# A two-layer decoder trunk on one core: a prefetch hint for the jump over a rarely taken branch, and another order of the expert groups around it

## The chip, the cores and the metric

The kernel runs on one core of a Trainium2 chip. The metric is the time of one execution in device microseconds (us); lower is better. The core has TensorE (PE for matmuls, PEld for the weight loads that run beside them), VectorE (DVE), ScalarE (ACT), GpSimd (POOL) and SyncE (SP); DMA queues move data between main memory and the on-chip memory.

## The reference

`reference()` runs two decoder layers over 256 tokens of width 1024 in float32. Layer 0 mixes tokens with a Mamba-2 block, layer 1 with block-sparse attention; neither is touched here. After each mixer comes the PEER channel mixer, and then a layer norm and a gated add:

```python
q = (xb @ w_q).reshape(PEER_TOKEN_BLOCK, PEER_HEADS, 2, PEER_HALF)
s = jnp.einsum('thcd,hcnd->thcn', q, sub_keys).astype(f32)
...                       # top 16 of 128 keys, twice; top 16 of their 256 sums
u_g = u[expert]
v_g = v[expert]
act = jax.nn.gelu(jnp.einsum('td,thkd->thk', xb, u_g).astype(f32))
return jnp.einsum('thk,thkd->td', (gate * act).astype(v_g.dtype), v_g)
...
x = layer_norm(alpha * x + ffn, ln_ffn_g[i], ln_ffn_b[i])
gate = jax.nn.sigmoid((x @ ple_w_gate[i]).astype(jnp.float32)).astype(x.dtype)
x = x + gate * (p[i] @ ple_w_proj[i])
```

Each layer has 16384 experts (a table u for the way in and a table v for the way out), and each token uses 8 x 16 of them.

## The kernel before

All of it is unrolled Python in a class `Net`; a tile framework turns data dependences into semaphores, and each engine runs its own instructions strictly in the order in which they were put on its queue. The change lies in the last part of `peer(i)`, which runs once for each layer.

**How the experts are worked.** The 16384 experts are 128 *columns* of 128. For every column, `expert_in` multiplies the tokens with the whole of u. The weights of the columns are kept in main memory (`table`; `first` holds those of the first block of tokens alone) for columns 0 to 95, and on the chip (the tile `high`) for columns 96 to 127. For the way out, columns 96 to 127 are *dense*: `dense(e)` takes column e of v by a plain DMA on SP's queue (512 KB) and multiplies it with the weights of all 256 tokens, 12 matmuls. Of columns 0 to 95 only the experts that some token uses are worked: they are sorted into *groups* of 128 rows, and `group(s)` fetches the rows of v and of the weight table by two indirect DMAs on POOL's queue (`fetched`). There are 84 groups: 38 whose experts are used by both blocks of 128 tokens (kind 0, the list `both`, 12 matmuls), 23 for the first block alone (kind 1, `one`, 6 matmuls) and 23 for the second alone (kind 2, `two`, 6 matmuls). The last five of `two` form the list `last` and are worked at the very end, so that the first block's layer norm can run beside them.

**What a column or a group costs.** float32 is multiplied as a high and a low part: `split` has ACT cast the high part (`hi`) and DVE subtract it for the low part (`lo`), once for the weights `w` (128 or 256 wide) and once for the 1024-wide rows of v, into a tile of the ring `hl` (4 buffers). PE then takes three products for each bank `acc`. The gathered rows stand in `raws` (a ring of 6 after the branch; before it two halves of `early` and a buffer of the ring `raw`) and `rows_w` (8). Dense columns and the gate's weights use the ring `raw` (4).

**The branch.** If a kind has more experts than its groups hold, `general()` works all 96 columns densely. With these inputs it is not taken. Each engine reads the flag (`values_load`) and jumps over the code of `general()`, which is 1153 instructions for PE alone in the built program, with as many weight loads beside the matmuls. In the skipped arm each engine raises its semaphore by what `general()` would have raised it.

**The order around it.** First 12 columns of `expert_in`, then 6 dense columns (`LEAD`), beside which DVE builds the groups' lists; then `mixed(one, ...)`, the 23 groups of kind 1 with 12 dense columns (`MIX`) spread evenly among them; the branch; `mixed(two, ...)`, 18 groups of kind 2 with the other 14 dense columns; the 38 groups of kind 0, beside which `weave` issues the loads of x, of the projection pp, of the norm's factors and of 7 of the gate's 8 weight tiles; then the five last groups. Their rows are fetched and split first (`group_load`, kept in `end`), four into `hl` and one into a quarter of a wide tile that is free until the gate's eighth tile needs it: the tile `high`, which held the dense columns' weights and is reused. Then the first block's layer norm is put down (`layer_norm`), and then the groups' matmuls, between which the normed block is turned by PE (`turn`, lines 186 to 189).

## Time and profile before

| | us |
|---|---|
| median of 3 runs | 1867.04 |
| lowest, highest | 1866.49, 1877.65 |
| the profiled execution, by its time | 1866.64 |
| its span, first to last instruction | 1864.8 |
| PE busy in it | 1812.8 (97%) |
| POOL busy in it | 633.4 (34%) |
| mean granted clock of TensorE | 0.990 |

The span and the time of the profiled execution differ by 1.8 us of start and end. A row of the timeline reads: start, duration, engine, line, operation, out<-in, count, and in brackets how long the engine had been idle and which instruction, by the semaphores, released it. "q" behind an engine is its sequencer, which runs jumps and waits. Layer 0's stage from the first dense column to the turned block is at about 667 to 948 us of the span, layer 1's at 1555 to 1835.

### The profile page before, as it was taken

The numbers are of one execution on the slowest core, as the hardware profiler recorded it, in microseconds if no ns is written. First come the engines' busy times: TensorE is split into PE (matmuls) and PEld (weight loads), VectorE is DVE, ScalarE is ACT, GpSimd is POOL, SyncE is SP. The second block draws the span as 40 slices with busy tenths as digits, with TensorE's granted clock in tenths as the row PEclk, the third lists the DMA queues.
The fourth block names the chain that finished last, engine by engine and source line by source line (L and its number), as shares of the span: only waits on it lengthen the run. The fifth ranks groups of instructions, "written<-read, shape, count | busy, mean of one in ns | idle before, by whom it ended". The sixth has DMA issues, their size and how long they took to land. (4 is left out here: it accounts for less than half of the span.)

```text
span 1864.8 us, 31726 instructions
## 1 busy us (share of the span) xinstructions
PE 1812.8 (97%) x11112; PEld 1541.5 (83%) x11112; DVE 1489.9 (80%) x2928; ACT 1153.5 (62%) x2330; POOL 633.4 (34%) x620
## 2 busy tenths in 40 slices
PE   9999999999999999899989999999999999989997
PEld 8998888888888877688868788888888887768886
DVE  7798789989989977676567778998998897667655
ACT  6865556696666656574446655669666665657543
POOL 0001013332222257767700001332222225776770
PEclk9999999999999999999989999999999999989999
DMA  7555669897699998997725556989779999889771
GB/s 279 197 180 191 210 186 227 218 251 193 184 283 331 286 278 284 322 363 259 225 90 192 203 188 182 227 219 249 192 184 286 322 285 289 279 310 364 237 234 49
DMA packets 217908, 444.32 MB, mean 238 GB/s; under 512 B 18980, under 2 KB 126664, under 8 KB 216072
## 3 DMA queue, kind: packets, MB, share of 16 engines
q1 hardware_dynamic: 75208, 266.75, 42.3%
q0 software_dynamic: 67648, 137.66, 28.8%
q10 hardware_dynamic: 74880, 37.75, 7.1%
q8 instruction: 91, 1.49, 0.3%
q14 instruction: 81, 0.66, 0.1%
HBM read 364.46 MB, written 44.08 MB: 219 GB/s over the span
## 5 line engine op out<-in xcount | busy, mean ns | idle before, releaser
L126 DVE TENSOR_TENSOR hl<-raw,hl 128x1024 fp32r<-128x1024 f32 x570 | 694.4, 1221 | 196.9 <-ACT hl L125 193.2
L162 PE MATMUL acc<-xT,hl 128*128 128x256 f32 (+1 forms) x4608 | 841.7, 340 | 1.6 <-DVE xT L189 0.8
L162 PEld LDWEIGHTS acc<-xT,hl 128*128 128x128 f32 x4608 | 701.0, 188 | 101.8 <-DVE hl L126 4.0
L125 ACT CAST hl<-raw 128x1024 fp32r<-128x1024 f32 x570 | 597.6, 1052 | 205.2 <-DMA raw<-in_v,r 83.1
L150 PE MATMUL acc<-hl,w 128*128 128x512 f32 x2220 | 522.6, 397 | 39.2 <-ACT hl L125 29.2
L150 PEld LDWEIGHTS acc<-hl,w 128*128 128x128 f32 x2220 | 422.6, 191 | 139.0 <-ACT hl L125 32.2
L919 POOL DMA_DIRECT2D w<-w x160 | 138.8, 868 | 404.2 <-ACT w L938 241.4
L919 POOL DMA_DIRECT2D act<-w x96 | 83.6, 871 | 303.2 <-ACT w L918 182.0
L1169 POOL DMA_INDIRECT raw<-in_v,r x136 | 142.8, 1050 | 65.5 <-issue 30.5
L917 ACT COPY w<-acc 128x256 f32<-128x256 f32 x160 | 59.9, 374 | 164.7 <-PE acc L162 155.2
L1169 POOL DMA_INDIRECT rows_w<-w_d,r x122 | 149.1, 1222 | 37.2 <-issue 36.6
L150 PE MATMUL mm<-xT,hl 128*128 128x256 f32 x816 | 100.9, 284 | 0.5 <-DVE hl L126 0.5
L150 PEld LDWEIGHTS mm<-xT,hl 128*128 128x128 f32 x816 | 98.6, 192 | 1.8 <-DVE hl L126 0.7
L918 ACT COPY w<-acc 128x256 f32<-128x256 f32 x256 | 97.4, 380 | 0.0
L917 ACT COPY act<-acc 128x256 f32<-128x256 f32 x96 | 35.7, 372 | 72.1 <-PE acc L162 71.8
L963 DVE TENSOR_TENSOR pick<-pick,r 128x2048 f16<-128x2048 f16 x64 | 78.2, 1222 | 1.0
L979 PEld LDWEIGHTS <-pick 128*128 128x128 f16 x1024 | 67.0, 98 | 12.8 <-issue 9.6
L215 POOL TENSOR_TENSOR ln_s<-ln_s,mhalf 128x1 f32<-128x1 f32 x8 | 4.4, 550 | 186.3 <-PE acc L150 130.5
L980 PE MATMUL mm<-pick 128*128 128x96 f16 x512 | 67.5, 206 | 0.0
L1169 POOL DMA_INDIRECT pick<-a_d,r x46 | 55.0, 1196 | 23.7 <-issue 13.1
L537 POOL TENSOR_TENSOR sq<-sq,sqt 128x256 f32<-128x256 f32 x12 | 12.5, 1039 | 147.9 <-ACT sqt L536 147.6
L126 DVE TENSOR_TENSOR hl<-pick,hl 128x1024 fp32r<-128x1024 f32 x32 | 39.3, 1228 | 27.0 <-ACT hl L125 25.9
(290 smaller groups left out, 2123.9 us busy)
## 6 DMA issues: line engine op xcount, KB each, us to landing
raw<-in_u SPq DMA_DIRECT2D x256, 512.0 KB, 4.8
raw<-in_v SPq DMA_DIRECT2D x64, 512.0 KB, 5.4
w_d<-act ACTq DMA_DIRECT2D x48, 512.0 KB, 8.7
w<-w POOLq DMA_DIRECT2D x160, 128.0 KB, 5.7
raw<-in_w_q SPq DMA_DIRECT2D x32, 512.0 KB, 3.9
raw<-in_w_xbc SPq DMA_DIRECT2D x24, 512.0 KB, 4.0
act<-w POOLq DMA_DIRECT2D x96, 128.0 KB, 5.1
a_d<-act ACTq DMA_DIRECT2D x24, 512.0 KB, 10.2
```

Source lines behind the costliest of these rows:

```text
L125: a = self.nc.scalar.copy(hi, src)
L126: b = self.nc.vector.tensor_tensor(lo, src, hi.bitcast(F32), op=OP.subtract)
L150: self.last_mm = self.nc.tensor.matmul(out, lhs(a), rhs(b), start=start and i == 0, stop=stop and i == 2).ins
L162: self.nc.tensor.matmul(dst, hl[:, a, k * P:(k + 1) * P], src, start=k + a == 0, stop=(k, a) == order[-1] and k == KD - 1)
L537: nc.gpsimd.tensor_tensor(self.sq[g], self.sq[g], t, op=OP.add)
L917: nc.scalar.copy(whole, pe[:, :T])
L918: copied = nc.scalar.copy(pair[:, 1, :], pe[:, T:]).ins
L919: nc.gpsimd.dma_start(whole, pair[:, 1, :], accum_op=OP.add)
L963: nc.vector.tensor_tensor(a2, both, gates, op=OP.mult)
L979: nc.tensor.matmul(pg[:, t, :], one[:, 0, 4 * h + t], a2[:, 4 * h + t, k], start=k == 0, stop=k == 1)
L980: nc.tensor.matmul(banks["used"][:, MANY * tb:MANY * tb + MANY], one[:, 0, 4 * h + t], a2[:, 4 * h + t, 0, :MANY], start=at == 0, stop=at ...
L1169: got = nc.gpsimd.indirect_dma_start(out=dst, out_offset=None, in_=src, in_offset=rows(which))
```

## The change

It makes these edits, in both layers:

- Six dense columns ahead of `one` become eight, and 11 instead of 12 are mixed with `one`, so 19 instead of 18 stand ahead of the branch and 13 instead of 14 behind it.
- PE, ACT and DVE get a branch prefetch hint three quarters of the way through `one`, and the two arms of the branch swap their places in memory: `general()` comes straight behind the compare, so that not taking it is now a taken jump to a short arm behind it, which the code that follows adjoins. Before, the short arm came straight behind the compare and ended in a jump over `general()`.
- Behind the branch, groups of kind 0 and 2 and the remaining 13 dense columns are mixed evenly (the dense ones over the first 72%), and the loads are placed among them by a table of positions: gate weights from 0.1 on. The gate's tiles are loaded in the order 0 to 6 instead of 0, 4, 1, 5, 2, 6, 3.
- Of the five last groups, the first instead of the fifth goes into the quarter of the wide tile.

```diff
--- before.py
+++ after.py
@@ -25,14 +25,13 @@
 PLAIN = range(6)
 TAIL = 5
 TURNS = (3, 4, 1, 2)
-ORDER = (0, 4, 1, 5, 2, 6, 3, 7)
 SPLIT = ((0, 0), (0, 1), (1, 0))
 MANY = 96
 ROUTED = 56
 GATED = 116
 DIRECT = ROUTED - 8
-LEAD = 6
-MIX = 12
+LEAD = 8
+MIX = 11
 CAPS = (38, 23, 23)
 BASES = (0, 38, 61)
 GROUPS = sum(CAPS)
@@ -1240,16 +1239,24 @@
                         todo.pop(0)()
             both, one, two = ([b + k for k in range(n)] for b, n in zip(BASES, CAPS))
             last, two = two[-TAIL:], two[:-TAIL]
-            closing = both[-1]
             early = [tl([P, 1536], F32, "pick", 2) for _ in range(2)]
             picked["n"], picked["order"] = -1, ()
 
-            def mixed(groups, columns):
-                place = lambda kind, l: [((k + 0.5) / len(l), kind, s) for k, s in enumerate(l)]
-                for _, kind, s in sorted(place(group, groups) + place(dense, columns), key=lambda p: p[0]):
-                    kind(s)
-
-            mixed(one, range(MANY + LEAD, MANY + LEAD + MIX))
+            def spread_over(f, l, upto=1.0):
+                return [(upto * (k + 0.5) / len(l), f, s) for k, s in enumerate(l)]
+
+            def emit(*steps):
+                for _, f, s in sorted(sum(steps, []), key=lambda step: step[0]):
+                    f(s)
+
+            def hint(_):
+                with self.after(self.pace.marks[1:] + (self.last_mm,)):
+                    self.tc.mark_branch_hint_location(f"over{i}", "LikelyTaken",
+                                                      [e.engine for e in (nc.tensor, nc.scalar, nc.vector)])
+
+            inner = sorted(spread_over(group, both) + spread_over(group, two), key=lambda step: step[0])
+            closing = [s for _, _, s in inner if s in both][-1]
+            emit(spread_over(group, one), spread_over(dense, range(MANY + LEAD, MANY + LEAD + MIX)), [(0.75, hint, None)])
             cells.__exit__(None, None, None)
             late_pool = stack.enter_context(self.tc.tile_pool(name=f"rest{i}", bufs=1))
             new = lambda shape, name, dt=F32: late_pool.tile(shape, dt, name=f"{name}{i}")
@@ -1259,29 +1266,31 @@
             wide = [new([P, 4, 2, 1024], "wide", F32R)]
             with self.after(self.pace.marks):
                 surplus = nc.values_load(picked["flag"][:1, :1], min_val=0, max_val=1)
-            with self.tc.If(surplus > 0, preferred_fallthrough_block=False):
+            with self.tc.If(surplus > 0, preferred_fallthrough_block=True, label=f"over{i}"):
                 general()
             self.pace.marks = ()
-            mixed(two, range(MANY + LEAD + MIX, P))
-            wide.append(tl([P, 4, 2, 1024], F32R, "high"))
             pgw = {}
 
-            def gate_load(n, tiles):
-                pgw[divmod(n, 4)] = self.chunk(dram["w_pg"][i, n], hl=tiles[:, n % 4])
-
-            self.weave([lambda s=s: group(s) for s in both],
-                       [lambda: nc.sync.dma_start(x, self.x_d[i]), lambda: nc.sync.dma_start(pp, self.pp_d[i]),
-                        lambda: self.load_gb(gb0, 2 * i + 1)]
-                       + [lambda n=n: gate_load(n, wide[n // 4]) for n in ORDER[:12 - TAIL]])
+            def gate_load(n):
+                if len(wide) <= n // 4:
+                    wide.append(tl([P, 4, 2, 1024], F32R, "high"))
+                pgw[divmod(n, 4)] = self.chunk(dram["w_pg"][i, n], hl=wide[n // 4][:, n % 4])
+
+            def extra(f):
+                with self.after(self.pace.marks):
+                    f()
+
+            loads = [(0.65, lambda: nc.sync.dma_start(x, self.x_d[i])), (0.7, lambda: nc.sync.dma_start(pp, self.pp_d[i])),
+                     (0.75, lambda: self.load_gb(gb0, 2 * i + 1))]
+            loads += [(at, lambda n=n: gate_load(n)) for n, at in enumerate((0.1, 0.25, 0.4, 0.55, 0.8, 0.87, 0.94))]
+            emit(inner, spread_over(dense, range(MANY + LEAD + MIX, P), 0.72), [(at, extra, f) for at, f in loads])
             end = []
             for k, s in enumerate(last):
-                n = ORDER[min(12 - k - 1, 7)]
-                end.append(group_load(s, None if k < 4 else wide[n // 4][:, n % 4]))
+                end.append(group_load(s, None if k else wide[1][:, 3]))
             dump = tl([P, D], F32, "pick", 2)
             gts = raws[:2]
             self.layer_norm(0, accs[0], x, gb0, gb1, dump, pool)
-            for n in ORDER[12 - TAIL:]:
-                pgw[divmod(n, 4)] = self.chunk(dram["w_pg"][i, n], after=(self.norm_marks[0][1],))
+            pgw[1, 3] = self.chunk(dram["w_pg"][i, 7], after=(self.norm_marks[0][1],))
             for k, (kind, w, hl) in enumerate(end):
                 group_out(kind, w, hl, (1,) if k == TAIL - 1 else ())
                 if k in TURNS[:2]:
```

Each of the following pieces stands on both layers alike; those of layer 0 are shown.

**PE at the branch, before.** The names are bank, tile of rows and tile of weights, with their numbers.

```order
L150 MATMUL acc_7959<-hl_8671,w_8672 128x512 x3
L150 MATMUL acc_7960<-hl_8671,w_8672 128x512 x3
L1261 TENSOR_LOAD r_902_7454
L1262 COMPARE_AND_BRANCH
L1262 UNCONDITIONAL_BRANCH
L150 MATMUL acc_7959<-hl_8721,w_8717 128x512
```

**PE at the branch, now.** The hint stands 24 rows of three matmuls ahead of the compare; the two pieces are the rows at the hint and those at the compare.

```order
L149 MATMUL acc_7959<-hl_8545,w_8546 128x512 x3
L149 MATMUL acc_7960<-hl_8545,w_8546 128x512 x3
L1427 BRANCH_PREFETCH_HINT
L149 MATMUL acc_7959<-hl_8563,w_8564 128x512 x3
L149 MATMUL acc_7960<-hl_8563,w_8564 128x512 x3
```

```order
L149 MATMUL acc_7962<-hl_8676,w_8672 128x512 x3
L149 MATMUL acc_7959<-hl_8694,w_8695 128x512 x3
L149 MATMUL acc_7960<-hl_8694,w_8695 128x512 x3
L1268 TENSOR_LOAD r_902_7454
L1269 COMPARE_AND_BRANCH
L149 MATMUL acc_7959<-hl_8744,w_8740 128x512
```

The last row of the first and of the third piece is the first matmul of `general()`, which is skipped: the jump over it has moved from behind the compare into the compare itself. The hint carries the line of the kernel's call.

**ACT behind the branch, before** (casts of the high parts; `rows_w` and `raw50`, `raw00` and so on are gathered groups, `high_332` and `raw_` with a number of its own a dense column):

```order
L1262 UNCONDITIONAL_BRANCH
L125 CAST w_1452_10925<-rows_w0_8693 128x128
L125 CAST hl_1451_10924<-raw50_8692 128x1024
L125 CAST w_1453_10936<-high_332_2361 128x256
L125 CAST w_1457_10959<-rows_w0_8693 128x128
L125 CAST w_1458_10970<-high_332_2361 128x256
L125 CAST w_1462_10993<-rows_w0_8693 128x128
L125 CAST hl_1455_10940<-raw_1454_10939 128x1024
L125 CAST hl_1456_10958<-raw00_8687 128x1024
```

**ACT behind the branch, now:**

```order
L124 CAST w_1455_10948<-rows_w0_8716 128x256
L124 CAST hl_1454_10947<-raw50_8715 128x1024
L124 CAST w_1456_10965<-high_332_2361 128x256
L124 CAST w_1460_10988<-rows_w0_8716 128x128
L124 CAST w_1462_11002<-rows_w0_8716 128x256
L124 CAST w_1464_11022<-rows_w0_8716 128x256
L124 CAST hl_1458_10969<-raw_1457_10968 128x1024
L124 CAST hl_1459_10987<-raw00_8710 128x1024
L124 CAST hl_1461_11001<-raw10_8711 128x1024
L124 CAST hl_1463_11021<-raw20_8712 128x1024
```

The first group is now one of kind 0 (256 wide), and ahead of the first dense column's rows stand the weights of four gathered groups instead of three.

**ACT at the last groups, before.** The five last groups are in `raw10`, `raw20`, `raw30`, `raw40` and `raw50`; the row of L204 is the first block's norm.

```order
L125 CAST w_1614_12249<-rows_w0_8693 128x128
L125 CAST hl_1613_12248<-raw10_8688 128x1024
L125 CAST w_1616_12257<-rows_w0_8693 128x128
L125 CAST high_1529_11454<-raw50_8692 128x1024
L125 CAST hl_1615_12256<-raw20_8689 128x1024
L125 CAST w_1618_12265<-rows_w0_8693 128x128
L125 CAST hl_1617_12264<-raw30_8690 128x1024
L125 CAST w_1620_12273<-rows_w0_8693 128x128
L125 CAST hl_1619_12272<-raw40_8691 128x1024
L125 CAST w_1621_12280<-rows_w0_8693 128x128
```

**ACT at the last groups, now:**

```order
L124 CAST high_1585_12020<-raw10_8711 128x1024
L124 CAST hl_1607_12197<-raw40_8714 128x1024
L124 CAST w_1610_12218<-rows_w0_8716 128x128
L124 CAST hl_1609_12217<-raw50_8715 128x1024
L124 CAST w_1612_12232<-rows_w0_8716 128x256
L124 CAST hl_1611_12231<-raw00_8710 128x1024
L124 CAST w_1613_12251<-rows_w0_8716 128x128
L124 CAST w_1615_12259<-rows_w0_8716 128x128
L124 CAST hl_1614_12258<-raw20_8712 128x1024
L124 CAST w_1617_12267<-rows_w0_8716 128x128
L124 CAST hl_1616_12266<-raw30_8713 128x1024
L124 CAST w_1619_12275<-rows_w0_8716 128x128
```

Before, the rows of the fifth of the last groups stood ahead of those of the second, third and fourth; now the rows of the first stand ahead of three groups that PE works before it, and the other four come in their own order.

## The prediction

> **What bounds the kernel now.** I read the page's first part, then the waits of PE and of POOL over the stage that the change touches, then the timeline at each long wait.
>
> ```profile
> span 1864.8 us, 31726 instructions
> PE 1812.8 (97%) x11112; PEld 1541.5 (83%) x11112; DVE 1489.9 (80%) x2928; ACT 1153.5 (62%) x2330; POOL 633.4 (34%) x620
> ```
>
> PE is busy for 97% of the span, so only its idle time can be won without less work. The waits of PE from the first group to the turned block, layer 0 and then layer 1:
>
> ```profile
> PE acc L150 <- ACT hl L125: 15.1, 3, 7.4
> PE acc L150 <- DVE hl L126: 3.1, 5, 0.8
> PE mm L186 <- DVE last L221: 0.4, 1, 0.4
> PE acc L150 <- ACT hl L125: 14.1, 4, 7.4
> PE acc L150 <- DVE hl L126: 3.0, 5, 0.8
> PE mm L186 <- DVE last L221: 1.6, 1, 1.6
> ```
>
> That is 18.6 and 18.7 us, 37.3 in all, in a few pieces. The second engine to watch is POOL, though the page gives it 34%. In the windows 746 to 934 us and 1637 to 1822 us, the gathers from the branch to the last groups:
>
> ```profile
> L1169 POOL DMA_INDIRECT rows_w<-w_d,r x61 | 75.5, 1237 | 18.6 <-issue 18.3 <-DMA raw<-in_v,r 0.3
> L1169 POOL DMA_INDIRECT raw<-in_v,r x61 | 63.1, 1034 | 30.2 <-issue 14.0 <-DVE hl L126 11.2 <-DVE w L126 3.4
> L1169 POOL DMA_INDIRECT rows_w<-w_d,r x60 | 72.7, 1211 | 18.3 <-issue 18.0 <-DMA raw<-in_v,r 0.3
> L1169 POOL DMA_INDIRECT raw<-in_v,r x60 | 62.1, 1035 | 30.8 <-issue 12.8 <-DVE hl L126 11.0 <-DVE w L126 5.4
> ```
>
> Busy and idle add up to 187.4 of 188 us in layer 0: POOL issues gathers without a break. Of its idle time, what DVE ended (11.2 + 3.4 = 14.6 us over ten instructions, 11.0 + 5.4 = 16.4 over thirteen) is waiting for a gather buffer; less 0.3 us of issue each, **11.6 and 12.5 us**. Without these a group costs (187.4 - 11.6) / 61 = 2.88 us of POOL, layer 1 2.86. PE's price, from this row,
>
> ```profile
> 827.10 73.08 PE L150 MATMUL acc<-hl,w 128*128 128x512 f32 x321 [0.67 <-DVE hl L126]
> ```
>
> is 73.08 / 321 = 0.228 us a matmul: 2.73 us for a dense column or a group of kind 0, 1.37 for one of kind 1 or 2. So the stage has two bounds that lie close together, and a term counts only as far as both allow. I make two sums for each layer and take the smaller gain.
>
> **PE's sum, first term: two more dense columns in front.**
>
> ```profile
> 684.60 1.04 ACT L125 CAST hl<-pick 128x1024 fp32r<-128x1024 f32 x1 [6.76 <-DMA pick<-in_v,r]
> 685.70 0.49 PE L150 MATMUL acc<-hl,w 128*128 128x512 f32 x1 [1.28 <-ACT hl L125]
> 686.96 9.38 PE L150 MATMUL acc<-hl,w 128*128 128x512 f32 x33 [0.77 <-DVE hl L126]
> 1578.95 0.50 PE L150 MATMUL acc<-hl,w 128*128 128x512 f32 x1 [0.96 <-ACT hl L125]
> 1580.21 17.07 PE L150 MATMUL acc<-hl,w 128*128 128x512 f32 x72 [0.76 <-DVE hl L126]
> ```
>
> PE runs out of dense columns before the first gather has landed. Two more are 2 x 2.73 = 5.5 us of cover, more than 1.28 + 0.77 and 0.96 + 0.76. Gain **2.0 and 1.7 us**; without that cover they are back. The dense column taken from the mix is no loss: 19 instead of 18 now stand ahead of the branch and 13 instead of 14 behind it.
>
> **Second term: the jump.**
>
> ```profile
> L1262 ACTq COMPARE_BRANCH  x4: 34/38/49, 751.3 to 1639.4; - x4
> L1262 PEldq COMPARE_BRANCH  x4: 81/3141/7168, 753.9 to 1643.3; - x4
> 756.14 0.30 ACT L125 CAST w<-rows_w 128x128 fp32r<-128x128 f32 x1 [4.70 <-DMA raw<-in_v]
> 756.35 1.04 ACT L125 CAST hl<-raw 128x1024 fp32r<-128x1024 f32 x1
> 758.85 2.94 ACT L125 CAST hl<-raw 128x1024 fp32r<-128x1024 f32 x3 [0.45 <-DMA raw<-in_v]
> 761.18 9.03 PE L150 MATMUL acc<-hl,w 128*128 128x512 f32 x29 [6.43 <-ACT hl L125]
> 1643.24 0.30 ACT L125 CAST w<-rows_w 128x128 fp32r<-128x128 f32 x1 [3.99 <-PEq L1262]
> 1643.45 1.04 ACT L125 CAST hl<-raw 128x1024 fp32r<-128x1024 f32 x1
> 1650.49 17.72 PE L150 MATMUL acc<-hl,w 128*128 128x512 f32 x64 [7.42 <-ACT hl L125]
> ```
>
> PE's rows name ACT as the releaser, but ACT had the first rows ready at 757.39 and 1644.49. What ended last is PE's own second jump, the one over `general()`, 7.17 us in layer 1. With the hint I expect it gone, but not the whole gap. Layer 1 shows what remains: PE stops at 1650.49 - 7.42 = 1643.07, ACT may cast only then (1643.24, released by PE's sequencer), and its rows are ready at 1644.49, some 1.6 us after PE stopped; DVE's low part needs 1.2 us more (below), of which four matmuls cover 0.9. That is 2 us. Next comes a dense column whose DMA is issued behind the branch. In layer 0 its cast began at 758.85; PE, which now stops at 754.75 + 2.73 - 2.0 and works 2.73 us of the first group, has it almost in time; I take 0.3. In layer 1 ACT must first cast the weights of the fourth gathered group:
>
> ```profile
> 1642.88 0.95 POOL L1169 DMA_INDIRECT rows_w<-w_d,r  x1 [0.30 <-issue]
> 1645.38 0.95 POOL L1169 DMA_INDIRECT rows_w<-w_d,r  x1 [0.31 <-issue]
> 1647.21 0.30 ACT L125 CAST w<-rows_w 128x128 fp32r<-128x128 f32 x1 [1.91 <-DMA rows_w<-w_d,r]
> ```
>
> The third group's weights landed 4.3 us after their start, so the fourth's at 1649.7 and the dense rows at 1650.9, against PE's 1643.07 + 2.73 - 1.7 + 2.0 + 2.73 = 1648.8: 2.1 us. So 2.3 and 4.1 us stay. Gain 6.43 - 2.3 and 7.42 - 4.1, **4.1 and 3.3 us**. A hint itself is in no row: I bound it between nothing and an ACT jump's 0.05 us and take nothing. SP has no hint; a jump of 5 us on it would lie under its wait for DVE.
>
> The same jump over 290 and more instructions of ACT lasts 0.05 us in its row, and ACT's next cast comes 4.70 us later: there the fetch shows as idle time. The Trainium skill, in "Runtime: NRT & Kernel Launch", section "Instruction fetch mechanics", says that prefetch is purely sequential and that a taken branch out of the window waits for a DMA fetch. PE's long jump agrees with it; by that rule alone the hint would change nothing, and the second term would be zero, which is the second rival.
>
> **Third term: the end.**
>
> ```profile
> 937.27 1.04 ACT L125 CAST high<-raw 128x1024 fp32r<-128x1024 f32 x1 [9.41 <-DMA raw<-in_v,r]
> 939.32 0.80 PE L150 MATMUL acc<-hl,w 128*128 128x512 f32 x1 [7.41 <-ACT hl L125]
> 948.05 0.66 PE L186 MATMUL mm<-ident,last 128*128 128x128 f32 x4 [0.39 <-DVE last L221]
> 1824.25 1.04 ACT L125 CAST high<-raw 128x1024 fp32r<-128x1024 f32 x1 [9.22 <-DMA raw<-in_v,r]
> 1826.29 0.80 PE L150 MATMUL acc<-hl,w 128*128 128x512 f32 x1 [5.32 <-ACT hl L125]
> 1827.81 0.68 DVE L200 SCALAR_TENSOR_TENSOR last<-last,acc 128x512 f32<-128x512 f32 x1
> 1832.06 1.41 DVE L213 SCALAR_TENSOR_TENSOR last<-last,ln_s,last 128x512 f32<-128x512 f32 x2
> 1835.03 0.66 PE L186 MATMUL mm<-ident,last 128*128 128x128 f32 x4 [1.60 <-DVE last L221]
> ```
>
> ACT and DVE stand 9 us at the fifth of the last groups, the last that POOL fetches; the second to fourth and the norm (L200 on) are queued behind it. From PE's stop (931.91, 1820.97) to the turned block (948.05, 1835.03) are 16.1 and 14.1 us, with 18 matmuls in them, 4.1 us: 12.0 and 10.0 us idle. Now each group is cast as it lands. If nothing is late, the norm starts with the last group of kind 0 and takes its 7.2 us (1827.81 to 1835.03), with two conversions between its steps as before, while PE has four groups, 5.5 us. With half a microsecond for the start, 2.2 us idle remain: gain **9.8 and 7.8 us**.
>
> PE's sum is 2.0 + 4.1 + 9.8 = **15.9** and 1.7 + 3.3 + 7.8 = **12.8 us**.
>
> **POOL's sum.**
>
> ```profile
> L126 DVE TENSOR_TENSOR hl<-raw,hl 128x1024 fp32r<-128x1024 f32 x570 | 694.4, 1221 | 196.9 <-ACT hl L125 193.2
> ```
>
> The last gather's landing to the turned block was 948.05 - 937.27 and 1835.03 - 1824.25, 10.8 us each. With the fifth group last in its queue there remain its cast (1.04), DVE's low part (1.2), the norm's two small sums (0.6, an estimate by the 0.68 of one L200), L213 (1.4) and the way from its end to the turn (1835.03 - 1833.47 = 1.6): 5.8 us. Gain 5.0. More must come from POOL's 11.6 and 12.5 us of buffer waits, for every gather starts later by what remains of them. Up to the last dense column PE works 13 + 29 pieces of 2.73 and 13 of 1.37 us, 132.5 us for 42 groups, 3.15 each, against POOL's 2.88: POOL may gain 42 x 0.27 = 11.3 us on PE. It starts some three groups ahead and six buffers hold three more, 3 x 2.88 = 8.6 us. So 3 to 4 us of waits stay; the ends are none and all, and I take 4. The last 14 groups and the five take PE 9 x 2.73 + 10 x 1.37 = 38.3 us and POOL 19 x 2.88 = 54.7, so 16 us of lead are used up there; six groups are 17. Gain 5.0 + 7.6 = **12.6** and 5.0 + 8.5 = **13.5 us**.
>
> The moved x, pp, norm and gate loads cost nothing while ACT and DVE, idle for 38% and 20% of the span, have them landed long before their cast: the ring `raw` lets SP run four loads ahead. Where one is late, ACT's queue stands still and the groups behind it wait, which costs nothing until PE has used up its four `hl` tiles, some 8 us.
>
> **Sum.** The smaller of the two is 12.6 and 12.8 us. The bounds lie so close that each will catch the other now and then; I take off 1.5 us a layer for that, an estimate from PE's small waits above (0.4 to 0.8 us each). 11.1 + 11.3 = 22.4 us off the profiled execution's 1866.64 (0.4 under the median) is **1844.2 us**, 1.2% under 1867.04. About 1% is what a measurement of this kernel can tell from no change, 1848.4 to 1885.7.
>
> **Rivals.**
> - *The gathers stay the bound.* If the even mix leaves the buffer waits at 11.6 and 12.5 us, only 5.0 a layer is won: 1856.6 us. For it: POOL never pauses today. Against: 3.15 against 2.88 us a group. Chance 0.20.
> - *The hint does nothing.* PE's sums fall to 11.8 and 9.5; less 1.5 each, 18.3 us: 1848.3 us. For it: the rule above. Against: each PE stop is exactly the jump. Chance 0.20.
> - *Slower.* Dense and gate loads now share the DMA queues with gathers all along. If a group then costs POOL more, every 0.1 us is 6.1 us a layer. From 2.88 + 12.6 / 61 = 3.09 us on, the gain is gone; at 3.4, 61 x 0.52 = 31.7 us less 12.6, 19 us a layer: 1905 us. Against: the row below, 800 to 836 us with the DMA queues full (share 1.00), gives 21.54 / 19 = 1.13 us a gather, no more than the (75.5 + 63.1) / 122 = 1.14 of the whole. Chance 0.07.
>
> ```profile
> 800.00:836.00 36.00, 35.33 (x156) 28.94 (x155) 28.01 (x36) 25.52 (x39) 21.54 (x19) 1.00 1.00 383
> ```
>
> **Numbers.** The forecast has 0.53; its own range is 1838 (no allowance, and the low end of the buffer waits) to 1849. The range down to 1837 and up to 1858 takes in the first two rivals and leaves out the third. Faster by over 1%: 0.48 of the forecast's and 0.10 of the second rival's chance, 0.58; slower 0.07; within 1% the other 0.35.
>
> **What would show it.** PE's compare at the branch under 0.3 us, and PE's gap there 2 to 4 us; no wait of PE at the first group; ACT's `high` cast of a gathered group no longer the last wait, and the turned block 6 us after the last landing; POOL's waits for DVE at about 4 us a layer. A jump of 6 us would show the second rival, buffer waits above 10 us the first. The forecast is wrong if ACT's four weight casts ahead of the first dense rows behind the branch or the first group's early `high` cast (it stands ahead of three groups) holds PE for more than the 1.5 us that I allow.

## The result, and the profile after

The changed kernel takes 1854.15 us (median of 7 runs, 1849.43 to 1860.54), the kernel before in the same comparison 1870.41 us (1866.49 to 1877.65): a ratio of 0.9913, 95% interval 0.9889 to 0.9937. That is 16 us off where 22 were forecast, inside the stated range and under the 1% that I had called the limit of a measurement. The profiled execution took 1854.15 us, 12.5 less than the profiled one of before. (Single executions of the changed kernel lie 11 us apart, and one of a kernel below took 4597.57 us, unexplained, and is in no ratio; so the pair of profiles is read for where time moved, and the medians and ratios for how much.)

The span, and then PE's waits from the first gathered group to the turned block, layer 0 and layer 1, as they were shown for the kernel before (us in total, times, longest):

```profile
span 1852.0 us, 31751 instructions
...
PE acc L149 <- ACT hl L124: 9.9, 4, 4.6
PE acc L149 <- DVE hl L125: 2.8, 5, 0.8
PE mm L185 <- DVE last L220: 0.4, 1, 0.4
...
PE acc L149 <- ACT hl L124: 8.0, 4, 4.2
PE acc L149 <- DVE hl L125: 3.0, 4, 0.9
PE mm L185 <- DVE last L220: 0.5, 1, 0.5
```

13.1 and 11.5 us, where it was 18.6 and 18.7: PE's waits fell by 12.7 us and the span by 12.8. What is left stands in two places, behind the branch and at the end.

**At the branch.** The rows of the branch's own line (compares, and the semaphore bump with which each engine leaves it; durations in ns, minimum, median and maximum, then the start in layer 0 and in layer 1), and the timeline of layer 0 behind it:

```profile
L1269 ACTq COMPARE_BRANCH  x2: 54/59/64, 753.8 to 1635.5; - x2
L1269 DVEq COMPARE_BRANCH  x2: 78/84/90, 754.8 to 1636.7; - x2
L1269 PEldq COMPARE_BRANCH  x2: 362/372/383, 756.1 to 1638.2; - x2
L1269 ACTq EVENT_SEMAPHORE  x2: 17/17/17, 757.0 to 1638.5; - x2
L1269 DVEq EVENT_SEMAPHORE  x2: 21/21/21, 757.8 to 1641.5; - x2
...
758.02 0.40 ACT L124 CAST w<-rows_w 128x256 fp32r<-128x256 f32 x1 [4.39 <-DVEq L1269]
759.42 0.64 PE L149 MATMUL acc<-hl,w 128*128 128x512 f32 x1 [2.42 <-ACT hl L124]
765.19 0.40 ACT L124 CAST w<-rows_w 128x256 fp32r<-128x256 f32 x1 [3.72 <-DMA rows_w<-w_d,r]
766.59 1.65 PE L149 MATMUL acc<-hl,w 128*128 128x512 f32 x3 [2.57 <-ACT hl L124]
```

PE's compare takes 0.37 us instead of 6 to 7. But ACT and DVE still need 3.0 to 4.8 us from their compare to their bump, and DVE's bump (757.8, 1641.5) is now what ACT's first cast waits for. SP waits for it too, before it issues the first dense column's DMA. Before, DVE bumped ahead of its jump over `general()`, 0.1 us behind the compare; with the arms swapped the bump stands in the arm that the jump leads to. DVE's bump and SP's DMA before, and SP's DMA now:

```profile
L1262 DVEq EVENT_SEMAPHORE  x2: 21/21/21, 752.7 to 1640.5; - x2
752.84 10.93 SPq L136 DMA_DIRECT2D raw<-in_v  x6
...
757.92 1.89 SPq L135 DMA_DIRECT2D raw<-in_v  x2
```

So the dense rows, which had landed at 758.75 us, land at 764.51 (both as the trace pairs DMAs with landings), and after one group, at 764.02, PE stops a second time for them. Their cast waits 1 us more behind a weight cast (765.19) whose gather has only then landed. In layer 0 the stops are 2.42 + 2.57 us against one of 6.43, in layer 1 2.96 + 0.36 against 7.42.

**At the end.** Layer 0's timeline: ACT's cast of the first of the last groups, PE's stop, the last gather and the turned block; then the last gather and the turned block of layer 1, and the two last gathers of the kernel before.

```profile
924.63 1.04 ACT L124 CAST high<-raw 128x1024 fp32r<-128x1024 f32 x1 [9.76 <-DMA raw<-in_v,r]
926.67 0.64 PE L149 MATMUL acc<-hl,w 128*128 128x512 f32 x1 [4.60 <-ACT hl L124]
932.03 1.23 POOL L1168 DMA_INDIRECT raw<-in_v,r  x1 [0.30 <-issue]
943.43 0.66 PE L185 MATMUL mm<-ident,last 128*128 128x128 f32 x4 [0.36 <-DVE last L220]
...
1811.94 1.22 POOL L1168 DMA_INDIRECT raw<-in_v,r  x1 [0.30 <-issue]
1822.20 0.65 PE L185 MATMUL mm<-ident,last 128*128 128x128 f32 x4 [0.50 <-DVE last L220]
...
932.54 0.94 POOL L1169 DMA_INDIRECT raw<-in_v,r  x1 [0.30 <-issue]
1819.71 0.94 POOL L1169 DMA_INDIRECT raw<-in_v,r  x1 [0.30 <-issue]
```

ACT still stands 9.76 us at the wide buffer's cast, now with three landed groups queued behind it. Yet from the last gather's issue to the turned block it is 11.4 and 10.3 us, where it was 948.05 - 932.54 = 15.5 and 15.3.

**POOL.** The 61 groups of layer 0 from the branch to the end of the stage (749 to 934 us), and the `raw` gathers of 60 groups of layer 1 (1634 to 1814 us); busy us, mean ns, then idle us ahead of them by what ended it:

```profile
L1168 POOL DMA_INDIRECT rows_w<-w_d,r x61 | 70.0, 1147 | 18.6 <-issue 17.7 <-DMA raw<-in_v,r 0.9
L1168 POOL DMA_INDIRECT raw<-in_v,r x61 | 67.9, 1113 | 28.0 <-DVE hl L125 11.3 <-issue 10.7 <-DMA raw<-in_v,r 3.0
L1168 POOL DMA_INDIRECT raw<-in_v,r x60 | 64.9, 1081 | 27.5 <-issue 13.1 <-DVE hl L125 10.2 <-DVE w L125 2.6
```

The gathers themselves take as long as before (in layer 0 70.0 + 67.9 us against 75.5 + 63.1). The idle time ahead of the `raw` gathers, less 0.3 us of issue each, is the wait for buffers: 28.0 - 18.3 = 9.7 and 27.5 - 18.0 = 9.5 us; by the same count it was 30.2 - 18.3 = 11.9 and 12.8. It has hardly fallen, and that is where the forecast's missing time is.

One more view explains a part of each stop. The windows behind PE's stop at the branch, of the kernel before and then of the changed one (window, length, busy time and count of PE, PEld, DVE, ACT, POOL, then PE's granted clock, DMA share, GB/s):

```profile
754.70:761.10 6.40, 0.05 (x1) 0.00 (x0) 3.77 (x8) 4.51 (x9) 4.88 (x6) 0.83 0.93 325
761.10:766.00 4.90, 4.82 (x12) 3.81 (x13) 3.10 (x4) 2.04 (x3) 3.98 (x4) 0.52 1.01 394
766.00:772.00 6.00, 6.00 (x28) 4.95 (x27) 3.59 (x6) 2.66 (x5) 4.78 (x5) 1.00 1.03 389
...
759.40:764.00 4.60, 4.58 (x12) 3.32 (x12) 2.19 (x4) 0.88 (x3) 3.68 (x4) 0.63 0.93 323
766.60:770.00 3.40, 3.40 (x8) 2.72 (x9) 3.40 (x3) 2.80 (x4) 2.89 (x2) 0.52 1.02 407
```

After a stop the granted clock is about half: 12 matmuls take 4.82 us and 8 take 3.40, where 28 take 6.00 at full clock. PE counts as busy in that time, so no wait shows it. A stop of 6.43 us cost some 2 us more than its gap (12 matmuls take 2.7 us at 0.228 us each), and each of the two stops of 2.5 us cost nearly as much again.

### The profile page after: what moved, and what is told of

It reads as the page before. It is cut to its first block, busy times and chain, and to the rows that moved or that the text cites. A ratio compares the mean times of both kernels' runs of the same rounds, so it can differ in the third digit from the quotient of the medians.

```text
span 1852.0 us, 31751 instructions
## 1 busy us (share of the span) xinstructions
PE 1811.4 (98%) x11112; PEld 1540.5 (83%) x11112; DVE 1490.5 (80%) x2928; ACT 1153.5 (62%) x2330; POOL 633.4 (34%) x620
## 5 line engine op out<-in xcount | busy, mean ns | idle before, releaser
L1168 POOL DMA_INDIRECT raw<-in_v,r x136 | 149.7, 1101 | 60.1 <-issue 28.3
L1168 POOL DMA_INDIRECT rows_w<-w_d,r x122 | 140.7, 1153 | 37.2 <-issue 35.1
L978 PEld LDWEIGHTS <-pick 128*128 128x128 f16 x1024 | 67.0, 98 | 12.8 <-issue 9.6
L1168 POOL DMA_INDIRECT pick<-a_d,r x46 | 58.0, 1262 | 23.7 <-issue 11.9
L536 POOL TENSOR_TENSOR sq<-sq,sqt 128x256 f32<-128x256 f32 x12 | 12.5, 1040 | 150.1 <-ACT sqt L535 149.9
```

The lines of the kernel that those rows point to most:

```text
L536: nc.gpsimd.tensor_tensor(self.sq[g], self.sq[g], t, op=OP.add)
L978: nc.tensor.matmul(pg[:, t, :], one[:, 0, 4 * h + t], a2[:, 4 * h + t, k], start=k == 0, stop=k == 1)
L1168: got = nc.gpsimd.indirect_dma_start(out=dst, out_offset=None, in_=src, in_offset=rows(which))
```

## The experiments

All times are medians, each ratio to the runs of the kernel before on the same chip, with its 95% interval.

| kernel | median, us | ratio to before |
|---|---|---|
| changed kernel | 1854.15 | 0.9913 (0.9889 to 0.9937) |
| branch alone, on before | 1872.29 | 0.9992 (0.9970 to 1.0014) |
| two dense columns ahead alone, on before | 1870.38 | 0.9989 (0.9965 to 1.0013) |
| wide buffer to the first alone, on before | 1867.51 | 0.9957 (0.9935 to 0.9980) |
| changed, no hint | 1853.31 | 0.9915 (0.9883 to 0.9946) |
| changed, wide buffer to the fifth | 1866.86 | 0.9962 (0.9941 to 0.9984) |
| changed, cast held in turn | 1858.98 | 0.9938 (0.9915 to 0.9962) |
| changed, five gather buffers | 1861.09 | 0.9936 (0.9911 to 0.9960) |
| changed, fewer weight gathers | 1840.38 | 0.9828 (0.9797 to 0.9860) |
| changed, dense over 0.90 | 1842.56 | 0.9845 (0.9816 to 0.9874) |
| dense over 0.90, cast in turn | 1837.52 | 0.9814 (0.9778 to 0.9849) |
| the same without the hint | 1838.33 | 0.9814 (0.9787 to 0.9841) |
| dense over 1.0, cast in turn | 1847.08 | 0.9861 (0.9833 to 0.9888) |

### The hint left out

```diff
-            emit(spread_over(group, one), spread_over(dense, range(MANY + LEAD, MANY + LEAD + MIX)), [(0.75, hint, None)])
+            emit(spread_over(group, one), spread_over(dense, range(MANY + LEAD, MANY + LEAD + MIX)))
```

> The changed kernel without the hint to the three engines; everything else is kept, the swapped arms of the branch too. Theory (the hint brings the code behind the jump to PE before PE gets there): PE's compare at the branch takes 6 to 7 us again instead of 0.37, the chunk of PE's code that arrived at 749.0 us, 7 us ahead of the compare, now arrives only behind it, PE's gap at the branch grows by about 5 us in each layer, and as PE is what the gathers wait for in the middle of the stage, little of it comes back: 1860 to 1864 us against 1854. Rival (the swap of the arms alone did it): the compare stays under 0.5 us and the time within 2 us of 1854.

Neither held. The rows of the branch's line without the hint:

```profile
L1269 DVEq COMPARE_BRANCH  x2: 63/68/72, 757.9 to 1636.3; - x2
L1269 PEldq COMPARE_BRANCH  x2: 4194/4243/4292, 759.3 to 1637.7; - x2
L1269 DVEq EVENT_SEMAPHORE  x2: 21/21/21, 762.6 to 1640.2; - x2
```

The hint does to PE what it says: without it the compare takes 4.2 us. (The swap of the arms alone brought it down from 6 to 7.) For DVE little changes, 4.7 and 3.9 us from compare to bump against 3.0 and 4.8 with the hint. And the time is the same: PE stops 4.10 and 4.36 us, once in each layer, where with the hint it stops 2.42 + 2.57 and 2.96 + 0.36. That is 8.5 us of stops without the hint and 8.3 with it: the second stop is what the first one hid. In both, SP issues the dense column's DMA only at DVE's bump (762.65 us here).

### The branch alone

```diff
-            mixed(one, range(MANY + LEAD, MANY + LEAD + MIX))
+            def hint(_):
...
+            for _, kind, s in sorted(place(group, one) + place(dense, range(MANY + LEAD, MANY + LEAD + MIX)) + [(0.75, hint, None)],
...
-            with self.tc.If(surplus > 0, preferred_fallthrough_block=False):
+            with self.tc.If(surplus > 0, preferred_fallthrough_block=True, label=f"over{i}"):
```

> The kernel before with nothing changed but the branch: the hint to PE, ACT and DVE three quarters through the first mix, and the swapped arms. Theory (the runs so far: without the hint the changed kernel took the same time, since PE's wait moves on to ACT's and DVE's own code and to the first dense column, each stop is followed by some ten matmuls at half the granted clock, and the gathers set the end): PE's compare falls from 6 to 7 us to 0.4, PE's stops there still add up to 3 to 5 us a layer, and the time stays at 1867 to 1871 us against 1870. Rival (the prediction's second term, 4.1 + 3.3 us): 1863 or less.

PE's compare fell to 0.37 and 0.57 us, and the time did not move: the theory, though the stops are longer in layer 0 than the 3 to 5 us that it names. PE's timeline behind the branch, in layer 0 and layer 1:

```profile
759.27 0.73 PE L150 MATMUL acc<-hl,w 128*128 128x512 f32 x2 [2.95 <-ACT hl L125]
760.53 1.38 PE L150 MATMUL acc<-hl,w 128*128 128x512 f32 x4 [0.53 <-DVE hl L126]
766.78 0.80 PE L150 MATMUL acc<-hl,w 128*128 128x512 f32 x1 [4.87 <-ACT hl L125]
...
1655.53 0.73 PE L150 MATMUL acc<-hl,w 128*128 128x512 f32 x2 [1.47 <-ACT hl L125]
1656.79 1.19 PE L150 MATMUL acc<-hl,w 128*128 128x512 f32 x4 [0.53 <-DVE hl L126]
1660.57 3.59 PE L150 MATMUL acc<-hl,w 128*128 128x512 f32 x13 [2.60 <-ACT hl L125]
```

The stops add up to 8.4 and 4.6 us: in layer 0 more than the 6.43 of before. Part of that is the swap's own doing: here too SP issues the first dense column's DMA at DVE's bump, at 757.89 us, where it was 752.84. The rest is a wait that the jump had covered.

### Two dense columns ahead, alone

```diff
-LEAD = 6
-MIX = 12
+LEAD = 8
+MIX = 11
```

> The kernel before with nothing changed but two more dense columns ahead of the first gathered group and one fewer in the first mix. Theory (the gathers decide, and they start no earlier): PE's waits at the first group (1.3 + 0.8 and 1.0 + 0.8 us) go, but come back as waits further on, 1869 to 1873 us against 1870 to 1873. Rival (the prediction's first term, 2.0 + 1.7 us, is won): 1867 or less.

The waits at the first group are gone, as they are in the changed kernel. A ratio of 0.9989 with 0.24% to either side does not tell the theory from the rival; the profiles of this kernel and of before are 2.8 us apart, no more than scatter.

### The wide buffer to the first, alone

```diff
-                end.append(group_load(s, None if k < 4 else wide[n // 4][:, n % 4]))
+                end.append(group_load(s, None if k else wide[n // 4][:, n % 4]))
```

> The kernel before with nothing changed but the wide buffer, given to the first of the last groups instead of the fifth. Theory (from the last gather's issue to the turned block 16.3 us with the fifth and 10.3 to 11.4 with the first, measured in the changed kernel): 5 us a layer, 1859 to 1862 us against 1870. Rival (it only moves ACT's standing queue three groups forward and PE's stop with it, so nothing is won): 1867 or more.

0.43% faster, 8 us of its own runs of the kernel before (1873.47 us here), 4 to 12 by the interval. The theory expected 8 us or more, the rival 3 or less, so the move wins time by itself, at the theory's near end. The profiled execution shows less of it: from the last gather's issue to the turned block it is 12.6 and 12.1 us (936.88 to 949.48 and 1821.96 to 1834.10), some 3 us a layer less than before and not 5. In layer 0 PE stops 5.84 us behind the standing cast and then, but for 0.65 us, has no idle time up to the turned block, so there PE sets the end.

### The wide buffer back to the fifth

```diff
-                end.append(group_load(s, None if k else wide[1][:, 3]))
+                end.append(group_load(s, None if k < 4 else wide[1][:, 3]))
```

> The changed kernel with the wide buffer given to the fifth of the last groups again; everything else is kept. Theory (moving it to the first moved the standing queue from the fourth and fifth groups to the three groups ahead, and won little): the turned block comes 10.8 us after the last landing as in the kernel before, but the last landing is 1.4 us earlier because POOL's buffer wait at the end goes: about 1 us a layer is lost, 1855 to 1857 us against 1854. Rival (the prediction's third term): 5 us a layer, 1864.

Here I had come to doubt the prediction's third term, wrongly. The last gather and the turned block of layer 1:

```profile
1822.73 0.94 POOL L1168 DMA_INDIRECT raw<-in_v,r  x1 [0.30 <-issue]
1838.98 0.44 PE L185 MATMUL mm<-ident,last 128*128 128x128 f32 x2 [0.74 <-DVE last L220]
```

16.3 us from the one to the other, against 10.3 in the changed kernel (in layer 0 16.3 against 11.4): 5 to 6 us a layer, and by the ratios 0.49% of the time. That is the rival, the prediction's own 5.0.

### The cast held in turn

```diff
+                own = hl is not None
                 kind, t, some, raw, hl = fetched(s, hl)
...
-                self.split(hl[:, 0], hl[:, 1], raw)
+                with self.after(picked["casts"] if own else ()):
+                    picked["casts"] = self.split(hl[:, 0], hl[:, 1], raw)
```

> The changed kernel, with the cast of the first of the last groups into the wide buffer held behind the cast of the group before it, on ACT and on DVE. Theory (ACT and DVE stand 9.8 us at that cast while three groups that have landed are queued behind it): PE's waits of 4.6 + 0.84 and 4.2 + 0.95 us at the end fall under 1 us, POOL's wait of 1.7 us there goes, and the turned block comes 4 to 5 us earlier after the stage's begin, since ACT's part of the norm then stands only behind the last landing: 1844 to 1846 us against 1854. Rival (the gathers bind here in any order): PE waits for each landing instead, and at most 2 us a layer are won, 1850 or more.

The 9.8 us of ACT and the 4.6 us stop of PE are gone, and nothing is won: the rival, the gathers bind. ACT's last cast, its part of the norm, and PE's turned block:

```profile
935.75 1.05 ACT L124 CAST hl<-raw 128x1024 fp32r<-128x1024 f32 x1 [2.07 <-DMA raw<-in_v,r]
938.22 1.15 ACT L203 ACTIVATE pick<-last,ln_s 128x1024 f32<-128x1024 f32 x1 [1.42 <-DVE ln_s L201]
941.31 0.90 PE L185 MATMUL mm<-ident,last 128*128 128x128 f32 x3 [5.08 <-DVE last L220]
```

PE uses the landed groups up sooner and then waits 5.08 us at the turned block, for a norm that is queued on ACT and DVE behind the casts of the last landing. Behind that stop its granted clock is 0.50, from 941.30 to 946.00 us. The stop was moved, not removed.

### Fewer weight gathers

```diff
-                for dst, src, which in ((some, values, "w"), (raw, dram["v"].rearrange("i e p d -> (i e p) d"), "v")):
+                for dst, src, which in ((some, values, "w"), (raw, dram["v"].rearrange("i e p d -> (i e p) d"), "v"))[n >= 70 and n % 2 == 0:]:
```

> The changed kernel with every second weight gather of the last 14 groups left out (7 of 168 gathers a layer; those groups use the weights that lie in the ring). POOL has 7 x 1.45 = 10 us less to issue at the end of each layer's stage; loads, casts and matmuls stay. Theory (POOL's gathers set the end of the stage): the turned block comes 5 to 8 us earlier in each layer, 1838 to 1845 us against 1854. Rival (PE, or ACT's order of casts, sets it): 2 us a layer at most, 1850 or more.

10 us less of POOL's work at the end of each layer made the kernel 0.85% faster than the changed kernel, some 14 to 16 us: the theory. The matmuls and the branch are as they were. The standing cast is not: with the gathers earlier, ACT stands 3.39 us at it in layer 0 (918.12 us) instead of 9.76, and PE's stop behind it is gone, though neither was touched. What the run takes away besides POOL's work is 7 landings that ACT's weight casts wait for; it does not separate the two. First gather to turned block, here and in the changed kernel:

```profile
673.48 1.30 POOL L1168 DMA_INDIRECT pick<-a_d,r  x1 [5.18 <-PE acc L149]
935.47 0.66 PE L185 MATMUL mm<-ident,last 128*128 128x128 f32 x4 [0.36 <-DVE last L220]
...
674.30 1.30 POOL L1168 DMA_INDIRECT pick<-a_d,r  x1 [5.18 <-DVE r L1131]
1555.62 1.36 POOL L1168 DMA_INDIRECT pick<-a_d,r  x1 [5.12 <-PE acc L149]
```

262.0 us against 943.43 - 674.30 = 269.1 in layer 0, and 261.6 against 266.6 in layer 1.

### Dense columns over 0.90 of the groups, alone and with the cast in turn

```diff
-            emit(inner, spread_over(dense, range(MANY + LEAD + MIX, P), 0.72), [(at, extra, f) for at, f in loads])
+            emit(inner, spread_over(dense, range(MANY + LEAD + MIX, P), 0.9), [(at, extra, f) for at, f in loads])
```

> The changed kernel with the dense columns behind the branch spread over 0.90 of the groups instead of 0.72. Theory (PE is the bound up to the last dense column and makes POOL wait 9.5 and 9.2 us for buffers, POOL is the bound behind it and starves PE): the buffer waits fall to 3 to 6 us, the last landing and with it the turned block come 3 to 6 us earlier, 1844 to 1849 us against 1854. Rival (later dense loads slow the gathers, or delay the last groups on PE by as much): 1852 or more.

The theory: 0.68% faster than the changed kernel. With the cast held in turn as well:

> The changed kernel with dense columns spread over 0.90 of the groups behind the branch, and the cast into the wide buffer held behind the cast of the group before it. Theory (the gathers decide when the last group lands, so ACT's standing queue costs only what PE has not yet used up, and that was 1.7 us of PE's waits with the later columns): 1840 to 1846 us, within 3 us of 1842.6. Rival (the standing queue is a cost of its own): 1838 or less.

1837.5 us, the fastest of all, 1.9% under the kernel before. It falls under what the theory named and just reaches the rival, but the two intervals (0.9816 to 0.9874, 0.9778 to 0.9849) overlap, so whether the cast in turn adds anything stays open. The `raw` gathers of 61 groups, first with 0.90 alone (layer 0, layer 1), then with both (layer 0, layer 1):

```profile
L1168 POOL DMA_INDIRECT raw<-in_v,r x61 | 69.9, 1146 | 26.2 <-issue 14.6 <-DVE w L125 8.3 <-DVE hl L125 2.3
L1168 POOL DMA_INDIRECT raw<-in_v,r x61 | 68.4, 1121 | 22.7 <-issue 14.3 <-DVE w L125 4.2 <-DVE hl L125 2.3
...
L1168 POOL DMA_INDIRECT raw<-in_v,r x61 | 68.8, 1128 | 18.6 <-issue 14.9 <-DMA raw<-in_v,r 2.1 <-DVE hl L125 1.2
L1168 POOL DMA_INDIRECT raw<-in_v,r x61 | 68.5, 1123 | 22.7 <-issue 14.6 <-DVE w L125 4.6 <-DVE hl L125 2.0
```

Less 18.3 us of issue, the buffer waits are 7.9 and 4.4 us with 0.90, and 0.3 and 4.4 with both, against 9.7 and 9.5. From 0.72 to 0.90 the time falls with them. With 0.90 alone, 3.4 of layer 0's 7.9 us are one wait at 923.82 us, behind the standing cast; with the cast in turn it is gone.

### Dense columns over all groups

```diff
-            emit(inner, spread_over(dense, range(MANY + LEAD + MIX, P), 0.9), [(at, extra, f) for at, f in loads])
+            emit(inner, spread_over(dense, range(MANY + LEAD + MIX, P), 1.0), [(at, extra, f) for at, f in loads])
```

> The changed kernel with dense columns spread over all groups behind the branch but the last five (1.0 instead of 0.72), and the cast into the wide buffer held behind the cast of the group before it. Theory (an even mix lets POOL run without buffer waits and PE without waits for gathers): buffer waits under 3 us a layer, 1832 to 1837 us against 1837.5 with 0.90. Rival (beyond 0.90 the dense loads and their casts stand in the way of the last groups): 1840 or more.

The rival, by the medians: slower than with 0.90 (intervals 0.9833 to 0.9888 and 0.9778 to 0.9849, just overlapping). The profiled execution does not show PE late: the turned block comes 5.6 us after the last landing in both layers, against 5.6 and 5.8 with 0.90 and the same cast. It is the last landing that comes later after the first gather, 261.4 and 256.2 us against 259.0 and 253.5. In layer 0 the last gather takes 7.37 us on POOL (at 923.29) where the others there take 0.9 to 2.0. A single long gather stands elsewhere in other profiles too (7.67 us at 677 us without the hint), so that may be chance, and layer 1 has none: why the landings come later stays open.

### Five gather buffers

```diff
-            raws = [new([P, 1024], f"raw{k}") for k in range(6)]
+            raws = [new([P, 1024], f"raw{k}") for k in range(5)]
...
-                    raw, some = raws[n % 6], rows_w[:, n % 8, :t]
+                    raw, some = raws[n % 5], rows_w[:, n % 8, :t]
```

> The changed kernel with five gather buffers instead of six; everything else is kept. Theory (the buffers are the lead that POOL carries over the last dense column into the stretch where it is the slower one): one group less of lead, 2.9 us a layer, 1858 to 1861 us against 1854. Rival (PE's part of the stage decides, and six buffers are more than it needs): 1852 to 1856.

The median is 7 us over the changed kernel's, the ratio 0.23% higher: what the theory expects in size, but the intervals overlap, so it only leans that way.

### The fastest version without the hint

```diff
-            emit(spread_over(group, one), spread_over(dense, range(MANY + LEAD, MANY + LEAD + MIX)), [(0.75, hint, None)])
+            emit(spread_over(group, one), spread_over(dense, range(MANY + LEAD, MANY + LEAD + MIX)))
```

> The version with dense columns over 0.90 and the ordered cast (1837.5 us), without the hint. Theory (without it PE's jump takes 4.2 us instead of 0.4, but ACT and DVE fetch their own code for 3 to 5 us beside it, and the gathers take up the rest): at most 3 us slower, 1837 to 1841 us. Rival (here, where the gathers wait less for buffers, the whole jump shows): 1843 or more.

The theory: 0.9814 with the hint and without.

## Why the prediction was right, and where it was wrong

The direction, the range and the frame held: two bounds close together, and the smaller gain decides. The size did not: 22.4 us were forecast, 16 measured (12 to 21 by the interval). That the range holds it is owed to the first rival, which the range was drawn to take in; the forecast's own range ended at 1849. And the prediction let PE's sum decide in layer 1, where it was POOL's as well.

- **First term.** No wait of PE at the first group, as forecast. Alone it gave nothing that can be measured.
- **The jump.** "I expect it gone, but not the whole gap" held, with compares of 0.37 us. The step that failed is layer 0's "almost in time; I take 0.3": PE stopped 2.57 us there. I had taken the dense rows' landing from the kernel before, but SP issues their DMA at DVE's bump, which the swapped arms had put behind the jump, 5 us later. The weight cast ahead of the rows, which I had counted in layer 1 alone, is the last 1 us of it. I had also not seen that each stop is paid a second time in half-clock matmuls. So the gap gave 1.4 instead of 4.1 us in layer 0 (before the half-clock matmuls, of which there are now two runs), 4.1 instead of 3.3 in layer 1, and the branch by itself was worth nothing measurable.
- **The end.** POOL's term, 5.0 us from last landing to turned block, held: counted from the last gather's issue it measured 4.1 and 5.1 (15.5 to 11.4, 15.3 to 10.3), and 5 to 6 when it was undone. By the landings that the trace pairs with the gathers, the block comes 10.8 us after the last one in both layers of all four kernels with the wide buffer at the fifth. In the changed kernel and the eight versions of it with the wide buffer at the first it comes 5.6 to 5.9 us after in 16 of 18 stages, where 5.8 were forecast; the other two are the changed kernel's layer 0 (6.8, where ACT's cast of the last group, at 937.66, waits for PE) and layer 1 without the hint (6.6). PE's term, 9.8 and 7.8 us, was not reached: the early `high` cast, which I had named as a danger, held PE for 4.6 + 0.84 us. But taking it out gained nothing, so PE's sum was not the one that counted. Part of what I called 12.0 us of idle time there was clock: PE's waits from 931.91 to 948.05 us are 7.41 + 0.65 + 0.39 = 8.5 us, and the 18 matmuls took the rest, with a granted clock of 0.50 from 939.30 to 945.50.
- **POOL's buffer waits.** This is the mis-sized term: "3 to 4 us of waits stay; I take 4". 9.7 and 9.5 us stayed (the sum as written leaves 11.3 - 8.6 = 2.7). Its two paces held: from 826.53 to 855.09 and on to 883.65 us POOL's gathers repeat every nine groups, 3.17 us a group with the waits and 2.82 without, against 3.15 and 2.88 in the sum. So what failed is what was set against their difference, the 8.6 us of lead. The sum has PE work without a stop, but PE's stops at the branch (5.0 us in layer 0, 3.3 in layer 1) and its half-clock matmuls behind them (some 3 us and 2 us) let POOL run that much further ahead: in layer 0 its buffers are full by 826 us, and it waits at PE's pace from there to the last dense column. With these the sum comes to 11 and 8 us of waits, against 9.7 and 9.5; that is arithmetic, and no run isolates it. Gain 2.2 and 3.3 us instead of 7.6 and 8.5.

With the measured terms POOL's sum is 4.1 + 2.2 = 6.3 and 5.1 + 3.3 = 8.4 us. From the first gather (672.76 and 1560.84 us before, 674.30 and 1555.62 after, below and above) to the turned block it was 275.3 and 274.2 us, and is 269.1 and 266.6: 6.2 and 7.6 us less. The sum closes to 0.1 and 0.8 us, in one execution of each kernel. It is the first rival's mechanism in the main (its sign, waits above 10 us, was just missed), and its 1856.6 us is nearer to 1854.15 than my 1844.2.

```profile
672.76 1.30 POOL L1169 DMA_INDIRECT pick<-a_d,r  x1 [5.18 <-DVE r L1132]
1560.84 1.36 POOL L1169 DMA_INDIRECT pick<-a_d,r  x1 [5.14 <-DVE r L1132]
```

The second rival fell as a mechanism, since the jump did go. That the hint is worth nothing in time was right for another reason: other waits stood under the jump, and one of them the swapped arms had made. The third did not occur, the gathers being no slower beside the dense loads. By parts, the ratios give 0.4 to 0.5% to the wide buffer, nothing measurable to the branch and to the two columns alone, and the rest, 0.4% or less, to the mix by difference only. That the gathers bind is shown in three ways: by fewer gathers (faster), by freeing PE and ACT at the end (not faster), and by the fixed time from the last landing to the turned block. In the changed kernel's layer 0 PE lies within about 1 us of them.

## What to carry to other kernels

Where two engines take turns as the bound within one stage, spread the work of the one over the work of the other before shortening any single wait: moving one number, 0.72 to 0.90, brought 0.68% where this whole change had brought 0.87%. How far to spread is to be tried, for 1.0 looked slower again. A long wait hides what stands under it, so before pricing its removal list everything that would be late next, on every engine that releases the one that waits. When the arms of a branch change places, see where each engine's semaphore bump then stands, and who waits for it. And test which of two close bounds decides by taking work from one of them alone.

## What the runs showed of the hardware

- After most stops of PE of 2 us and more the granted clock was about 0.5 (0.52 behind the 6.43 us and the 2.57 us stop above), in the changed kernel until 3.3 to 7.0 us behind the stop's end. Matmuls of 512 columns then start 0.43 us apart instead of 0.23. Worked out from the starts of single matmuls, five of the returns to full clock in the changed kernel are at 763.17, 770.04, 933.80, 1555.08 and 1811.09 us: 2, 50, 232 and 307 times 3.413 us behind the first, to within 0.05 us. So the clock changes on a fixed grid that runs on its own, and how long a stop is punished depends on where it falls. The Trainium skill, "TensorE: Matmul & The Clock Gate", section "What's actually happening", describes such a free-running window of 3413 ns; the runs agree with it on the grid, and show half clock after stops shorter than one window.
- A branch hint shortened PE's jump over a long arm from 4.2 to 0.37 us (3.9 to 4.3 and 0.36 to 0.57 over all runs); in the changed kernel without the hint, its arms swapped, it took 4.2 us where it had taken 6 to 7 before. On ACT and DVE the same hint made no difference that the traces show: from compare to bump 2.2 to 5.5 us in the runs with it, 2.5 to 5.3 in the two without.
